# Moving the DRAM weight sums of a hybrid mLSTM / sparse-attention block from the projection strips into attention, in another order of steps

## The chip, the core and the metric

The kernel runs on one core of a Trainium2 chip. The metric is device time in microseconds of one execution; a measured kernel has several runs, and their median is compared. The engines are named as the profile names them: PE is the tensor engine (PEld its weight loads), DVE the vector engine, ACT the scalar engine, POOL the GpSimd engine. SP issues DMAs and computes nothing; POOL issues DMAs too, beside its own computing. Times in the stages are us from the start of the profiled span.

## The reference

One layer of a decoder block on x of 512 tokens by 1024 channels, all in fp32:

```python
hN = _rmsnorm(x, norm_g[l])
p = _split_in(hN @ w_in[l])          # one projection, cut into q, k, v, o, z, gates, ...
mh = _mlstm(silu(conv(p["m_q"])), silu(conv(p["m_k"])), p["m_v"], i_gate, f_gate)
ya = sigmoid(p["m_o"]) * _head_layernorm(mh) * silu(p["m_z"])
yb = _nsa(q, compressed, selected, window, gates) * silu(p["n_z"])
merged = sigmoid(p["g_a"]) * (ya @ w_branch_a) + sigmoid(p["g_b"]) * (yb @ w_branch_b)
x = x + merged @ w_out
return _rmsnorm(x, final_norm_g)
```

The mLSTM branch has 4 heads of 256; the attention branch has 8 query heads of 64 in 2 groups. What matters here is four products of a 512 x 1024 matrix with a 1024 x 1024 weight: the projections to v, o and z, and the last one with w_out.

## The kernel before, in words

Every fp32 operand of a product is split into a high and a low part, and a product is three matmuls (high x high, high x low, low x high). A weight goes by `weights()`: SP loads 512 KB of it into a raw tile `wr` of which there are three; ACT copies the high part into `wh` (also three), DVE subtracts and writes the low part `wl` (three). A raw buffer is loaded again when DVE is done with it, and a `wh` is written again when PE is done with it.

The four big products are made in a form of Strassen's: quarters of the weight are added and subtracted, so that seven products of quarters stand for eight. The sums of weight quarters are made by DMA in DRAM, with no engine computing. A sum has two steps, each of two DMAs of 512 KB: `begin_sum` (SP, line 929) copies a quarter of the weight into a DRAM tile, `wsumv1` to `wsumv4` for v, `wsumo1` to `wsumo4` for o, `wsumout1` to `wsumout4` for w_out. `add_to_sum` (POOL, line 935) then adds another quarter, or another sum, to it: sum 2 adds sum 1, and sum 4 adds sum 2. z's sums are made on DVE from tiles `E` and `F` instead.

The 24 steps are called chores and stand in one list, `chores`; the places in the program at which the next one is taken set where its DMAs stand in the queues of SP and POOL. A chore's DMAs are kept in program order among themselves and with other pinned instructions; instructions that are not pinned are put by the scheduler of the framework where it likes.

The stages, by the span of the profile:

- to about 93: norm, keys and values, first gates and convolutions; two chores are taken here.
- attention, about 93 to 272: 16 units (query pair, head, branch). A unit's scores are made on PE, exponentiated on ACT, scaled on POOL (tile `P`, five instructions a unit), transposed on PE and multiplied with the values. Between them PE is fed from a stream of projection jobs (queries, convolutions q and k, gates), each with one weight. One chore is taken at the start of each unit, in the units 0 to 13.
- the strips, about 272 to 398: the projections to v, o and z, in 21 products of quarters. PE is fed from weights alone here: 12 matmuls for a 512 KB weight. `Strip` names what is done after each product; a table `then` of o and z took four chores in all, after one product of o and three of z.
- the heads, about 398 to 520: four mLSTM heads, with branch products in the stream; one chore a head. POOL computes one small power `rlr` a head.
- the end, 520 to 600: merge, the product with w_out, norm and stores.

Of the kernel before, what the change touches and what calls it, by code (L numbers as in the profile page):

```python
# [89 lines left out]
def build(  # L90
# [3 lines left out]
    nc = tc.nc  # L94
# [717 lines left out]
    def query_heads(c):  # L812
        H, L, *turned = roped.pop(("q", c))
        q = rope_b(*turned)
        Th = []

        def part(hh):
            s = slice(hh * 64, hh * 64 + 64)
            o = slice((1 - hh) * 64, (1 - hh) * 64 + 64)
            t = rpp.tile([128, T], F32R, name="Th", tag=f"Th{hh}")  # L820
            A(t[s, :], q[s, :], AF.Copy)
            dve.tensor_tensor(t[o, :], q[s, :], f(t[s, :]), OP.subtract)
            Th.append(t)

        heads[c] = H, L, Th
        return part
# [91 lines left out]
    def quarters(w, c0):  # L918
        return [[w[:, 4 * i : 4 * i + 4, c0 + 512 * j : c0 + 512 * j + 512] for j in range(2)] for i in range(2)]

    wov = w_out[0].rearrange("(k p) c -> p k c", p=128)
    parts_of = {"v": quarters(wv, MV), "o": quarters(wv, MO), "z": quarters(wv, MZ), "out": quarters(wov, 0)}
# [15 lines left out]
    def chores_of(w):  # L938
        (b11, b12), (b21, b22) = parts_of[w]
        return [  # L940
            lambda: begin_sum(w, 1, b11),
            lambda: begin_sum(w, 3, b12),
            lambda: begin_sum(w, 2, b22),
            lambda: begin_sum(w, 4, b21),
        ], [
            lambda: add_to_sum(w, 1, b12),
            lambda: add_to_sum(w, 3, b22),
            lambda: add_to_sum(w, 2, wsum[w, 1]),
            lambda: add_to_sum(w, 4, wsum[w, 2]),
        ]  # L950

    begun, added = zip(*(chores_of(w) for w in ("v", "o", "out")))
    (c1, c3, c2, c4), (a1, a3, a2, a4) = begun[2], added[2]
    chores = deque(begun[0] + added[0] + begun[1] + added[1] + [c1, c2, a1, a2, c3, a3, c4, a4])

    def next_chore():
        chores.popleft()()
# [173 lines left out]
    def new_p():  # L1131
        return (
            at.tile([128, 1280], F32, name="P", tag="P", bufs=3),
            at.tile([128, 8, NT], F32, name="st", tag="st", bufs=4),
        )
# [22 lines left out]
    def turn(n, i, P, kbs):  # L1158
        c, hh, b = units[i]

        def job():
            for kb, tt in ptrans(P, kbs).items():
                applying.setdefault(n + AFTER[kb], []).append(lambda kb=kb, tt=tt: apply(c, hh, b, kb, tt))

        turning.setdefault(n, []).append(job)
# [12 lines left out]
    for i, (c, hh, b) in enumerate(units):  # L1178
        cur = pair[b]
        if b and i + 1 < 16:  # L1180
            pair = new_p(), new_p()
        if i % 4 == 2 and c < 3:
            while ("q", c + 1) not in roped:
                stream.step(1)
            now["rp"] = lambda c=c: now.__setitem__("th", query_heads(c + 1))
            now["c"] = lambda c=c: side.append(compressed(c + 1))
            at_place("u")
        if i == 0:
            side.append(mgate())
        if i < 14:  # L1190
            next_chore()
        for j, kbs in enumerate(((0,), (1,), (2, 3))):
            turn(n + LATER + j, i, cur[0], kbs)
        for g in range(NT):
            if i + 1 < 16:
                score(*units[i + 1], g, pair)
            for job in turning.pop(n, ()):
                job()
            for job in applying.pop(n, ()):
                job()  # L1200
            n += 1
            if g % 2 == 0:
                continue
            for w in PLACES[g]:
                at_place(w)
            for _ in range(4):
                tick(FILL)
# [22 lines left out]
    def vals(h):  # L1230
        return yah[:, h, : NT * 258].rearrange("p (b d) -> p b d", b=NT)
# [12 lines left out]
    gate = gtp.__enter__().tile([128, NT, D], F32, name="gate")  # L1244
# [15 lines left out]
    E = st.tile([128, 4, 512], F32, name="E")  # L1260

    def piece_of(src, q):
        return src[:, 2 * q : 2 * q + 2]
# [59 lines left out]
    F = {}  # L1323

    def z_first(q):
        nc.sync.dma_start(piece_of(E, q), piece_of(parts_of["z"][0][0], q))
        return halves_of(piece_of(E, q))

    def z_sum1(q):
# [155 lines left out]
    def fetch_decay(h):  # L1485
# [1 line left out]
        tc.keep_in_program_order(nc.sync.dma_start(decays["g", h], decayed[h].partition_broadcast(128)))  # L1487

    sv = Strip("v", put_values)
    so = Strip("o", put_o, lambda l: gate[:, l, 512:], {5: next_chore})  # L1490

    sz = Strip(
        "z", put_z, None,
        {
            1: next_chore,
            2: next_chore,
            5: lambda: fetch_qk(0, (0,)),
            6: lambda: [fetch_decay(h) for h in (0, 1)],
            3: next_chore,
            7: lambda: fetch_qk(0, (1,)),  # L1500
        },
    )
# [99 lines left out]
    for h in range(4):  # L1602
        (qh, ql), (kh, kl) = tiles_of[0, h], tiles_of[1, h]
        vh, vl = vals(h), vals_low(h)
        Dm = decays.pop(h)
        Sh = mp.tile([128, 1280], F32R, name="Sh", tag="Sh")
        Sl = mp.tile([128, 1280], F32R, name="Sl", tag="Sl")
        for sb in range(NT):
            o, n = KOFF[sb], 512 - sb * 128
            pss = PT() if sb < 2 else PS()  # L1610
            ss = slice(sb * 128, sb * 128 + 128)
            mm3(
                pss[:, :n], lambda k: kh[:, k, ss], lambda k: kl[:, k, ss],
                lambda k: qh[:, k, sb * 128 :], lambda k: ql[:, k, sb * 128 :], range(2),
            )
            dv = Dm[:, o : o + n]
            dve.scalar_tensor_tensor(dv, pss[:, :n], 0.015625, dv, OP.mult, OP.mult)
            split(dv, Sh[:, o : o + n], Sl[:, o : o + n])
        stream.step(24)
        if h < 3:  # L1620
            fetch_qk(h + 1)
            if h < 2:
                fetch_decay(h + 2)
        chores.popleft()()
        if h == 3:
            mqp.__exit__(None, None, None)
            fetch_first()
        num = mp.tile([128, NT, 258], F32, name="num", tag="num")
        bs = mp.tile([128, NT, 6], F32, name="bs", tag="bs")
        mv = mp.tile([128, NT, 2], F32, name="mv", tag="mv")  # L1630
        for tb in range(NT):
            po = PT() if tb < 2 else PS()
            for sb in range(tb + 1):
                a = KOFF[sb] + (tb - sb) * 128
                lh, ll = Sh[:, a : a + 128], Sl[:, a : a + 128]
                pe.matmul(po[:, :258], lh, vh[:, sb, :], start=sb == 0, stop=False)
                pe.matmul(po[:, :256], lh, vl[:, sb, :], start=False, stop=False)
                pe.matmul(po[:, :258], ll, vh[:, sb, :], start=False, stop=sb == tb)
            A(num[:, tb], po[:, :258], AF.Copy)
            dve.bn_stats(bs[:, tb], num[:, tb, 0:256])  # L1640
            dve.bn_aggr(mv[:, tb], bs[:, tb])
        stream.step(24)
        rho = mp.tile([128, NT], F32, name="rho", tag="rho")
        va = mp.tile([128, NT], F32, name="va", tag="va")
        A(rho, num[:, :, 256], AF.Abs)
        dve.tensor_tensor(rho, rho, em[:, :, h], OP.max)
        dve.reciprocal(rho, rho)
        dve.tensor_tensor(va, rho, rho, OP.mult)
        dve.tensor_tensor(va, va, mv[:, :, 1], OP.mult)
        dve.tensor_scalar(va, va, EPS, None, OP.add)  # L1650
        r = rsqrt(mp, va, NT, "rl")
        dve.tensor_tensor(rho, rho, r, OP.mult)
        nb = mp.tile([128, NT], F32, name="nb", tag="nb")
        dve.scalar_tensor_tensor(nb, mv[:, :, 0], -1.0, rho, OP.mult, OP.mult)
        for tb in range(NT):
            nt = num[:, tb, 0:256]
            A(nt, nt, AF.Identity, bias=nb[:, tb : tb + 1], scale=rho[:, tb : tb + 1])
            dve.tensor_tensor(nt, nt, gate[:, tb, h * 256 : h * 256 + 256], OP.mult)
        if h < 3:
            decay(h + 1)  # L1660
        stream.step(NORM_FILL)
        for e in range(2):
            pt = PT()
            for tb in range(NT):
                pe.transpose(
                    pt[:, tb * 128 : tb * 128 + 128], num[:, tb, e * 128 : e * 128 + 128], ident
                )
            ct = h * 2 + e
            gain = prm[:, ct, 10:11]
            A(ya(ct), pt, AF.Copy, scale=gain)  # L1670
            dve.scalar_tensor_tensor(yal[:, ct], pt, gain, f(ya(ct)), OP.mult, OP.subtract)
        stream.step(12)
# [321 lines left out]
```

## Time and profile before

| | us |
|---|---|
| median of 3 runs | 601.69 (600.55 to 602.02) |
| the profiled execution's own time | 602.6 |
| its span, first to last instruction | 600.5 |
| PE busy | 585.8 (98%) |
| DVE busy | 459.0 (76%) |
| ACT busy | 363.5 (61%) |
| POOL busy | 121.4 (20%) |
| mean granted clock | 0.995 |

A busy PE is not PE at its peak: matmuls overlap and their ends are modelled, so the start of one matmul to the start of the next tells more than its length. In a list of waits, "A <- B: 3.4, 1, 3.4" reads: A waited for B 3.4 us in total, once, 3.4 at the longest. In a row of the timeline stand start, length, engine, line, operation, what it writes and reads, how many instructions are merged in the row, and in brackets how long the engine idled before and what ended that. In a table of stretches, the DMA share is the mean busy share of the 16 DMA engines.

### The profile page before, as it was taken

Reading aid. Unit: us, or ns where it says so; the run is one execution under the profiler, and the core shown is the slowest. Engines: PE = TensorE matmul, PEld = TensorE weight load, DVE = VectorE, ACT = ScalarE, POOL = GpSimd, SP = SyncE. Lnnn points to the kernel's source line nnn. Section 1 sums busy time; section 2 is a strip of 40 time slices with the busy share of each in tenths; the row PEclk is TensorE's granted clock in tenths of the full one; section 3 lists DMA queues with packets and bytes.
Section 4 is the critical chain, followed back from the end, with each engine's and each line's share of the span. In section 5 each row is a group of like instructions: output and inputs, shape, how many; then the busy total and the mean of one; then the engine's idle time right before and its main releaser. Section 6 shows DMA issues by size and latency. Waiting matters only on the chain.

```text
span 600.5 us, 8563 instructions
## 1 busy us (share of the span) xinstructions
PE 585.8 (98%) x2896; PEld 491.5 (82%) x2896; DVE 459.0 (76%) x863; ACT 363.5 (61%) x662; POOL 121.4 (20%) x196
## 2 busy tenths in 40 slices
PE   8999999999999999999999799999999999999995
PEld 6898888888888888878888577888888888888884
DVE  4897669978869779887976376878767666679885
ACT  6848746676666667675765355576655542644544
POOL 5420601436323245440000110000200010001011
PEclk9999999999999999999999989999999999999999
DMA  8944995688993498874687886965996698767733
GB/s 319 330 115 134 279 245 146 194 197 197 229 260 111 134 225 180 202 170 130 220 278 231 227 204 188 300 178 164 335 271 224 207 276 265 246 205 260 239 103 141
DMA packets 102276, 128.47 MB, mean 214 GB/s; under 512 B 6228, under 2 KB 63188, under 8 KB 102232
## 3 DMA queue, kind: packets, MB, share of 16 engines
q1 hardware_dynamic: 96184, 112.78, 60.0%
q0 software_dynamic: 5760, 14.75, 14.5%
q8 instruction: 23, 0.38, 0.3%
q10 hardware_dynamic: 288, 0.39, 0.2%
q14 instruction: 21, 0.17, 0.1%
HBM read 109.61 MB, written 42.02 MB: 253 GB/s over the span
## 4 chain that ended last, share of the span: by engine, by line
PE 80%; DVE 9%; DMA 6%; ACT 4%; issue 2%; DVEq 0%; ACTq 0%
PE pp L234 11%; PE pp L232 11%; PE pp L230 11%; DMA wr<-w_in 4%; PE pp L1365 3%; PE pp L484 3%; PE pp L1367 3%; PE pp L1363 3%; PE pt L1097 2%; DVE wl L105 2%; PE pp L1720 2%; PE pp L1718 2%; PE pp L1722 2%; DMA wr<-wsumo 1%; DVE u L105 1%
## 5 line engine op out<-in xcount | busy, mean ns | idle before, releaser
L105 DVE TENSOR_TENSOR wl<-wr,wh 128x1024 fp32r<-128x1024 f32 (+3 forms) x103 | 122.3, 1190 | 58.5 <-ACT wh L105 57.3
L105 ACT ACTIVATE wh<-wr 128x1024 fp32r<-128x1024 f32 (+3 forms) x104 | 105.8, 1020 | 70.2 <-PE pp L232 18.0
L232 PE MATMUL pp<-hTl,wh 128*128 128x512 f32 x320 | 126.1, 394 | 0.0
L230 PE MATMUL pp<-hTh,wh 128*128 128x512 f32 x320 | 126.0, 394 | 0.0
L234 PE MATMUL pp<-hTh,wl 128*128 128x512 f32 x320 | 125.6, 393 | 0.0
L105 POOL TENSOR_SCALAR P<-P,st,gates 128x128 f32<-128x128 f32 (+2 forms) x80 | 53.5, 678 | 123.9 <-DVE st L105 117.3
L234 PEld LDWEIGHTS pp<-hTh,wl 128*128 128x128 f32 x320 | 60.1, 188 | 11.8 <-DVE wl L105 0.3
L230 PEld LDWEIGHTS pp<-hTh,wh 128*128 128x128 f32 x320 | 60.2, 188 | 11.3 <-ACT wh L105 0.2
L232 PEld LDWEIGHTS pp<-hTl,wh 128*128 128x128 f32 x320 | 60.2, 188 | 11.1
L105 ACT ACTIVATE P<-P,st 128x128 f32<-128x128 f32 (+3 forms) x64 | 35.6, 557 | 20.0 <-DVE st L105 19.7
L105 DVE SCALAR_TENSOR_TENSOR u<-pp,cst,u 128x511 f32<-128x511 f32 (+2 forms) x48 | 35.6, 741 | 1.5 <-ACT u L105 1.4
L105 ACT ACTIVATE pth<-pt 128x384 fp32r<-128x384 f32 (+1 forms) x48 | 24.9, 521 | 17.4 <-PE pt L1097 17.1
L105 DVE TENSOR_TENSOR ptl<-pt,pth 128x384 fp32r<-128x384 f32 (+1 forms) x48 | 28.4, 594 | 6.8 <-ACT pth L105 6.7
L105 DVE CUSTOM_DVE_ANT_0 P<-ps,cst 128x128 f32<-128x128 f32 (+3 forms) x64 | 30.2, 480 | 2.8 <-PE ps L1078 2.6
L105 POOL TENSOR_TENSOR rlr<-va,mhalf 128x4 f32<-128x4 f32 x4 | 4.1, 1032 | 137.7 <-DVE va L105 137.7
L1097 PE MATMUL pt<-cst,P 128*128 128x128 f32 x160 | 25.4, 273 | 0.0
L1097 PEld LDWEIGHTS pt<-cst,P 128*128 128x128 f32 x160 | 19.8, 140 | 4.4 <-DVE ptl L105 0.8
L1108 PE MATMUL po<-pth,vsw 128*128 128x512 f32 (+1 forms) x64 | 21.8, 350 | 0.8 <-ACT pth L105 0.6
L1363 PE MATMUL pp<-wh,S 128*128 128x512 f32 x48 | 19.5, 406 | 3.0 <-ACT wh L105 3.0
L1365 PE MATMUL pp<-wl,S 128*128 128x512 f32 x48 | 19.5, 406 | 1.7 <-DVE wl L105 1.7
L1367 PE MATMUL pp<-wh,S 128*128 128x512 f32 x48 | 19.4, 405 | 0.0
L1109 PE MATMUL po<-ptl,vsw 128*128 128x512 f32 (+1 forms) x64 | 19.3, 327 | 0.0
(429 smaller groups left out, 1408.0 us busy)
## 6 DMA issues: line engine op xcount, KB each, us to landing
wr<-w_in SPq DMA_DIRECT2D x60, 512.0 KB, 5.8
qk<-hl SPq DMA_DIRECT2D x16, 512.0 KB, 3.9
qk<-qk SPq DMA_DIRECT2D x16, 512.0 KB, 6.5
away<-s SPq DMA_DIRECT2D x16, 256.0 KB, 2.6
wsumv<-w_in SPq DMA_DIRECT2D x8, 512.0 KB, 7.0
wsumo<-w_in SPq DMA_DIRECT2D x8, 512.0 KB, 6.3
wr<-wsumv SPq DMA_DIRECT2D x8, 512.0 KB
wr<-wsumo SPq DMA_DIRECT2D x8, 512.0 KB, 6.5
```

Of the source, the lines that this page charges most:

```text
L105: ins = fn(*args, **kw)
L230: pe.matmul(ps, a, c, start=k == 0, stop=False)
L232: pe.matmul(ps, a, d, start=False, stop=False)
L234: pe.matmul(ps, b, c, start=False, stop=k == nk - 1)
L484: pe.matmul(keys_in[c], (b if p == 2 else a)[:, cs_], xl[k] if p == 1 else xh[k], start=k == 0 and p == 0, stop=k == ND - 1 and p == 2,)
L1097: pe.transpose(pt[:, n : n + 128], P[:, POFF[qb] + kb * 128 : POFF[qb] + kb * 128 + 128], ident)
L1108: pe.matmul(po[:, kb * 128 :], vl, th, start=b == 0 and kb == 0, stop=False)
L1109: pe.matmul(po[:, kb * 128 :], vl, tl, start=False, stop=False)
L1363: pe.matmul(ps, a, c, start=begin, stop=False, skip_group_check=not first)
L1365: pe.matmul(ps, a, d, start=False, stop=False, skip_group_check=not first)
L1367: pe.matmul(ps, b, c, start=False, stop=k == 3, skip_group_check=not first)
L1718: pe.matmul(ps, p, ya(k), start=k == 0, stop=False)
```

## The change

The list of chores is put in another order, and the places where a chore is taken change. In attention the units 1, 3, 5 and 7 take two, the others one, unit 15 none: 19 in place of 14. The strips take none. The heads take what is left, one each in the first three: the copy for w_out's sum 4, and the additions to its sums 2 and 4. In the list the additions for v, o and w_out stand mixed with the copies of the next weight. The two loads of `E` are pinned to program order.

```diff
     begun, added = zip(*(chores_of(w) for w in ("v", "o", "out")))
-    (c1, c3, c2, c4), (a1, a3, a2, a4) = begun[2], added[2]
-    chores = deque(begun[0] + added[0] + begun[1] + added[1] + [c1, c2, a1, a2, c3, a3, c4, a4])
+    (v1, v3, v2, v4), (o1, o3, o2, o4), (c1, c3, c2, c4) = begun
+    (va1, va3, va2, va4), (oa1, oa3, oa2, oa4), (a1, a3, a2, a4) = added
+    chores = deque(
+        [v1, v3, v2, v4, va1, va3, va2, o1, va4, o3, o2, o4, oa1, oa3, oa2, c1, oa4, c2, c3, a1, a3, c4, a2, a4]
+    )
...
-        if i < 14:
+        for _ in range(2 if i in (1, 3, 5, 7) else i < 15):
             next_chore()
...
     def z_first(q):
-        nc.sync.dma_start(piece_of(E, q), piece_of(parts_of["z"][0][0], q))
+        tc.keep_in_program_order(nc.sync.dma_start(piece_of(E, q), piece_of(parts_of["z"][0][0], q)))
...
-    so = Strip("o", put_o, lambda l: gate[:, l, 512:], {5: next_chore})
+    so = Strip("o", put_o, lambda l: gate[:, l, 512:])
...
-            1: next_chore,
-            2: next_chore,
             5: lambda: fetch_qk(0, (0,)),
             6: lambda: [fetch_decay(h) for h in (0, 1)],
-            3: next_chore,
             7: lambda: fetch_qk(0, (1,)),
...
-        chores.popleft()()
+        if chores:
+            next_chore()
```

On PE, DVE and ACT the instructions stand in the same order as before. On SP and POOL they don't; three places follow.

SP in the strips, from o's second product on (`wr` is a raw weight tile, `wsumo2` and its like the sums in DRAM, `E` z's first weights). Before:

```order
L170 DMA wr_3542<-wsumo2_2237 128x1024
L170 DMA wr_3562<-wsumo2_2237 128x1024
L929 DMA wsumout1_3583<-w_out 128x2x512 x2
L170 DMA wr_3586<-w_in 128x2x512
L170 DMA wr_3604<-w_in 128x2x512
L170 DMA wr_3625<-wsumo3_2120 128x1024
L170 DMA wr_3643<-wsumo3_2120 128x1024
L170 DMA wr_3665<-wsumo4_2365 128x1024
L170 DMA wr_3671<-wsumo4_2365 128x1024
L170 DMA wr_3741<-w_in 128x2x512
L170 DMA wr_3761<-w_in 128x2x512
L929 DMA wsumout2_3783<-w_out 128x2x512 x2
```

Now:

```order
L170 DMA wr_3555<-wsumo2_1860 128x1024
L170 DMA wr_3575<-wsumo2_1860 128x1024
L170 DMA wr_3596<-w_in 128x2x512
L170 DMA wr_3614<-w_in 128x2x512
L170 DMA wr_3635<-wsumo3_1857 128x1024
L170 DMA wr_3653<-wsumo3_1857 128x1024
L170 DMA wr_3675<-wsumo4_1983 128x1024
L170 DMA wr_3681<-wsumo4_1983 128x1024
L1329 DMA E_3154<-w_in 128x2x512 x2
L170 DMA wr_3751<-w_in 128x2x512
L170 DMA wr_3771<-w_in 128x2x512
```

Both copies for w_out are gone from here, and E's two loads, which stood among v's first loads, come behind o's last.

SP in attention, behind the turning of the third query pair (`rot1`; `away` and `qk` are stores of gates and of convolved q and k). Before:

```order
L320 DMA rot1_88<-rw_1772 8x512
L170 DMA wr_2101<-w_in 128x8x128
L929 DMA wsumo3_2120<-w_in 128x2x512 x2
L364 DMA away6944_0_1889<-s_1887 128x512
L929 DMA wsumo1_1974<-w_in 128x2x512 x2
L170 DMA wr_2205<-w_in 128x8x128
L170 DMA wr_2276<-w_in 128x8x128
L682 DMA qk01_1971<-hl_1968 256x1x512
```

Now:

```order
L320 DMA rot1_88<-rw_1777 8x512
L929 DMA wsumo3_1857<-w_in 128x2x512 x2
L929 DMA wsumo2_1860<-w_in 128x2x512 x2
L364 DMA away6944_0_1898<-s_1896 128x512
L929 DMA wsumo4_1983<-w_in 128x2x512 x2
L170 DMA wr_2110<-w_in 128x8x128
L170 DMA wr_2215<-w_in 128x8x128
L170 DMA wr_2285<-w_in 128x8x128
L682 DMA qk01_1980<-hl_1977 256x1x512
```

Three copies for o stand together, and the weight load that was ahead of them is behind them.

POOL from the last unit of attention into the heads (`P` the scaled scores, `yah` the values' ones, `rlr` a head's power). Before:

```order
L105 TENSOR_SCALAR P_2864<-P_2864,st_2865,gates_70 128x384
L105 TENSOR_SCALAR P_2866<-P_2866,st_2867,gates_70 128x128
L105 TENSOR_SCALAR P_2866<-P_2866,st_2867,gates_70 128x256
L105 TENSOR_SCALAR P_2866<-P_2866,st_2867,gates_70 128x384
L105 TENSOR_SCALAR P_2866<-P_2866,st_2867,gates_70 128x128
L105 TENSOR_SCALAR P_2866<-P_2866,st_2867,gates_70 128x384
L105 MEMSET yah_3113 128x4 x8
L935 DMA wsumout1_3583<-w_out 128x2x512 x2
L935 DMA wsumout2_3783<-wsumout1_3583 128x1024 x2
L105 TENSOR_TENSOR rlr_4347<-va_4340,mhalf_68 128x4
L935 DMA wsumout3_4252<-w_out 128x2x512 x2
L105 TENSOR_TENSOR rlr_4647<-va_4640,mhalf_68 128x4
```

Now:

```order
L105 TENSOR_SCALAR P_2875<-P_2875,st_2876,gates_70 128x384
L935 DMA wsumout3_2761<-w_out 128x2x512 x2
L105 TENSOR_SCALAR P_2877<-P_2877,st_2878,gates_70 128x128
L105 TENSOR_SCALAR P_2877<-P_2877,st_2878,gates_70 128x256
L105 TENSOR_SCALAR P_2877<-P_2877,st_2878,gates_70 128x384
L105 TENSOR_SCALAR P_2877<-P_2877,st_2878,gates_70 128x128
L105 TENSOR_SCALAR P_2877<-P_2877,st_2878,gates_70 128x384
L105 MEMSET yah_3126 128x4 x8
L105 TENSOR_TENSOR rlr_4350<-va_4343,mhalf_68 128x4
L935 DMA wsumout2_2635<-wsumout1_2374 128x1024 x2
L105 TENSOR_TENSOR rlr_4650<-va_4643,mhalf_68 128x4
L935 DMA wsumout4_4255<-wsumout2_2635 128x1024 x2
```

The additions for w_out's sums 1 and 3 are issued in attention (the one for sum 1 a unit earlier), the latter ahead of the last unit's scalings; the other two follow in the heads. Elsewhere in attention the additions for v and o stand earlier in POOL's queue than before, and o's first two, sums 1 and 3, stand next to each other behind unit 7's scalings, with the one for sum 2 behind unit 8's.

## The prediction

> **What bounds the kernel now.** I read the page's first part, then the busy times of each engine cut by stage (columns: stretch, length, busy us and instruction count of PE, PEld, DVE, ACT, POOL, then granted clock, DMA share, GB/s).
>
> ```profile
> PE 585.8 (98%) x2896; PEld 491.5 (82%) x2896; DVE 459.0 (76%) x863; ACT 363.5 (61%) x662; POOL 121.4 (20%) x196
> ...
> 95.00:275.00 180.00, 179.20 (x956) 151.14 (x955) 150.49 (x356) 119.86 (x267) 68.78 (x96) 1.00 0.74 181
> ...
> 340.00:350.00 10.00, 6.27 (x20) 4.48 (x19) 4.25 (x5) 4.01 (x6) 0.00 (x0) 0.83 0.62 191
> ...
> 372.00:376.00 4.00, 3.01 (x14) 2.15 (x13) 4.00 (x5) 2.66 (x4) 0.00 (x0) 1.00 0.38 86
> ...
> 400.00:520.00 120.00, 120.00 (x630) 103.09 (x628) 84.48 (x189) 64.22 (x126) 8.17 (x8) 1.00 0.84 255
> ```
>
> TensorE bounds nearly all of it. Attention (95 to 275) has 0.8 us of PE idle, the heads (400 to 520) none. The one hole is in the strips: 3.73 us at 340 to 350 with the clock at 0.83, and 0.99 us at 372 to 376. The order of instructions on PE, DVE and ACT is the same in both kernels; only SP and POOL issue in another order. So the change can give back what those holes cost and can take what it puts into attention, nothing else. What PE's weight loads waited for after 275, then PE's own rows around the holes, and the clock in the stretch behind the first:
>
> ```profile
> PEld pp L1363 <- ACT wh L105: 3.4, 1, 3.4
> PEld pp L1365 <- DVE wl L105: 2.5, 2, 1.4
> ```
> ```profile
> 335.62 0.39 PE L1363 MATMUL pt<-wh,S 128*128 128x512 f32 x1
> ...
> 340.86 0.39 PE L1367 MATMUL pp<-wh,S 128*128 128x512 f32 x1
> 344.23 0.50 PE L1363 MATMUL pp<-wh,S 128*128 128x512 f32 x1 [2.97 <-ACT wh L105]
> 345.49 0.55 PE L1365 MATMUL pp<-wl,S 128*128 128x512 f32 x1 [0.76 <-DVE wl L105]
> ...
> 349.24 0.40 PE L1365 MATMUL pp<-wl,S 128*128 128x512 f32 x1
> ...
> 373.03 0.39 PE L1363 MATMUL pp<-wh,S 128*128 128x512 f32 x1
> 374.41 0.50 PE L1365 MATMUL pp<-wl,S 128*128 128x512 f32 x1 [0.99 <-DVE wl L105]
> ```
> ```profile
> 345.81:349.22 3.41, 3.41 (x9) 2.67 (x8) 2.65 (x4) 1.86 (x3) 0.00 (x0) 0.50 0.71 167
> ```
>
> From 335.62 to 340.86 there are 23 steps, 5.24 / 23 = 0.228 us each: the undisturbed cadence of a 512-column matmul. At 340.86 it breaks, and once PE runs again, nine steps (345.49 to 349.24) go at half clock. What made the weights late is in the chain of waits (start, us, what):
>
> ```profile
> 324.31 7.60 DMA wr<-w_in
> 331.99 1.07 ACT wh L105
> 333.09 1.24 DVE wl L105
> 334.34 8.67 DMA wr<-wsumo
> ...
> 361.98 7.65 DMA wr<-w_in
> ```
>
> A weight buffer is loaded, split on ACT (1.07) and DVE (1.24), and there are three of them. Each holds 12 matmuls, 12 x 0.228 = 2.73 us of PE; three give 8.2 us a turn, so a load keeps up while it lands within 8.2 - 2.31 = 5.9 us. These landed in 7.6 to 8.7. How loads land without and with the weight sums (first row 285 to 321, second 321 to 345; the last figure is the median us to landing), and the sums' issues on SP and on POOL:
>
> ```profile
> wr<-wsumo SPq DMA_DIRECT2D x3, 512.0 KB, 4.4
> ...
> wr<-wsumo SPq DMA_DIRECT2D x5, 512.0 KB, 8.7
> ```
> ```profile
> 321.69 1.29 SPq L929 DMA_DIRECT2D wsumout<-w_out  x2
> 348.23 1.22 SPq L929 DMA_DIRECT2D wsumout<-w_out  x2
> ```
> ```profile
> 329.62 2.42 POOL L935 DMA_DIRECT2D wsumout<-w_out  x2 [51.34 <-DMA wsumout<-w_out]
> 355.03 0.83 POOL L935 DMA_DIRECT2D wsumout<-wsumout  x1 [22.99 <-DMA wsumout<-w_out]
> ```
>
> The load at 324.31 was issued 2.6 us behind the first copy, the loads at 334.34 and 361.98 4.7 and 7.0 us after POOL began a sum. That is the whole hole.
>
> **The change part by part.** *Strips.* Two copies and two sums leave 321 to 367. Freed of them, loads should land as at 285 to 321, in about 4.4, under 5.9. The cost that goes, term by term: 344.23 - 340.86 - 0.228 = 3.14; 345.49 - 344.23 - 0.228 = 1.03; nine steps at half clock, 3.75 - 9 x 0.228 = 1.70; 374.41 - 373.03 - 0.228 = 1.15. Sum **7.02 us**. Next to be late is nothing in the DMA: PE's own cadence. For the half clock, the Trainium skill ("TensorE: Matmul & The Clock Gate", Part 1) says that the array falls to half rate after an idle window of about 3.4 us and stays there for about one; the trace agrees (one stretch of 3.41 at 0.50). By that rule a hole that only shrinks below a window would lose no half clock, and the 1.70 would be kept even then.
>
> *E.* The 1 MB of z's first weights was fetched at 280 and is now issued behind the last load of o's sums, which stood at 337.58 of the old clock. Its row:
>
> ```profile
> E<-w_in SPq DMA_DIRECT2D x2, 512.0 KB, 4.7
> ```
>
> It lands near 343. PE, without the holes, wants it 43 matmuls after 340.86, at 350.7; less both splits (2.31), 348.4. Even at 8.7 it is in time. But it shares the engines with o's last loads, so I leave a residual of **0.3**. Its bounds are 0 and 4: the 55 us from 321 to 376 are 6.7 turns of 8.2, and each falls 0.6 short if loads land at the median that the page has for o's sums over the whole kernel, 6.5 rather than 5.9:
>
> ```profile
> wr<-wsumo SPq DMA_DIRECT2D x8, 512.0 KB, 6.5
> ```
>
> *Attention, DMA.* Three copies (3.15 MB) and two sums (2.1 MB) come in. The queues there and the weights:
>
> ```profile
> q1 hardware_dynamic: 24880, 24.03, 43.6%
> q0 software_dynamic: 3328, 8.39, 30.2%
> ...
> wr<-w_in SPq DMA_DIRECT2D x21, 512.0 KB, 4.8
> wsumo<-w_in POOLq DMA_DIRECT2D x4, 512.0 KB, 9.4
> ```
>
> 43.6% of 180 us for 24.03 MB is 3.27 us/MB, 30.2% for 8.39 MB is 6.48. So 3.15 x 3.27 + 2.1 x 6.48 = 23.9 us of 180: DMA share 0.74 to 0.87. The Trainium skill ("DMA: Bandwidth & Descriptors", Issuing engines are not separate DMA queues) speaks against the change: work issued from SP and from POOL ends on the same 16 engines, so moving it saves none. The trace agrees that both queues draw on one budget (43.6% and 30.2% make the 0.74).
>
> What decides is the room. In attention a weight is used every 180 / 21 = 8.6 us, so three buffers give 25.7 a turn where the strips give 8.2; 25.7 - 2.31 leaves 23 us for a landing, against 9.4 for a sum's own. Of the 30 waits listed for this stretch none has a DMA as releaser; ACT's weight splits wait for PE alone:
>
> ```profile
> ACT wh L105 <- PE pp L232: 7.7, 6, 1.8
> ```
>
> One load is moved directly: it stood ahead of o's copies and is now behind three of them and a store. The load, the store, and the split that I count as that load's own (loads and splits paired backward from the strips):
>
> ```profile
> 159.59 0.39 SPq L170 DMA_DIRECT2D wr<-w_in  x1
> ...
> 166.25 0.34 SPq L364 DMA_DIRECT2D away<-s  x1
> ...
> 183.04 1.05 ACT L105 ACTIVATE wh<-wr 128x1024 fp32r<-128x1024 f32 x1
> ```
>
> Issued near 168 and landing within 10 it is there at 178, 5 us early. Cost **0**; without that cover a late load costs its lateness.
>
> *Attention, POOL.* A pair of sum issues holds POOL 2.42 (row at 329.62). What queues behind it are P's scalings, for which PE's transposes wait.
>
> ```profile
> 184.01 1.09 POOL L105 TENSOR_SCALAR P<-P,st,gates 128x128 f32<-128x128 f32 x2 [0.83 <-DVE st L105]
> 193.16 2.69 POOL L105 TENSOR_SCALAR P<-P,st,gates 128x128 f32<-128x128 f32 x5 [8.06 <-DVE st L105]
> 205.43 2.15 POOL L105 TENSOR_SCALAR P<-P,st,gates 128x128 f32<-128x128 f32 x3 [9.58 <-DVE st L105]
> ...
> 265.80 3.49 POOL L105 TENSOR_SCALAR P<-P,st,gates 128x128 f32<-128x128 f32 x5 [1.56 <-DVE st L105]
> ```
>
> Four issues in a row now stand after 185.10: 4.84 into an idle 8.06, hidden with 3.2 over. Only the last sum, ahead of the last unit's scalings at 265.80, does not fit: POOL idles 1.56, the pair takes 2.42, so P is 0.86 late, and there PE has little else to fill with. The cost is between 0 (the first of the five took long anyway) and 0.9; I take **0.3**.
>
> *Heads.* Two copies and two sums become one copy and two sums. PE idles nowhere from 400 to 520 although two sums land there now: **0**, bounds 0 to 0.5.
>
> Sum: -7.02 + 0.3 + 0.3 = **-6.4**. Profiled: span 600.5, own time 602.6, so 594.1 and 596.2. The median of the runs is 601.69; on that, **595.3**.
>
> **Rivals.** *Half rescue.* The strips get lighter but loads still land near 6 to 7, since E moves in among o's last loads and z's fetches stay. For it: the 6.5 above. Against: 4.4 at 285 to 321, though F's 1 MB was fetched there. With 3 us of residual instead of 0.3 the sum is -7.02 + 3.0 + 0.3 = -3.7: **598**.
>
> *Attention takes it back.* The sums fill the DMA engines until weights come late. For it: the 0.74 that is there already. Against: 0.87 is still under 1, with 23 us of room for a landing. To come out as no change it must cost some 6 of the 7: 601.7 - 7.0 + 6.2 = **600.9**. The rule of the Trainium skill named above is the case for this one.
>
> *POOL blocks: slower.* The sum of o2 reads what the first of the four sums in a row wrote. In POOL's order it waits for that landing right after the scalings of 193.16 and holds back the next unit's. With a landing of 9.4 it waits not at all. The next unit's scalings start at 205.43; less 1.6 to issue the pair, a landing later than 203.8, which is 18.7 after 185.1, makes P late and PE with it. To end over 0.3% slower it must return 7.0 + 1.8 = 8.8 us: a landing 27.5 us after issue, three times the row. At 30 the price is 11.3, less 7.0: **606**.
>
> **How the numbers follow.** Forecast 79%, half rescue 11%, taken back 6%, slower 4%. 0.3% of 601.7 is 1.8 us, about what a measurement tells from no change: faster 0.90, same 0.06, slower 0.04. The gain's bounds: all 7.02 and a little of the run's spread gives 593.8; the high end reaches past the half rescue with its residual at the full 4, 599.
>
> **What would show it.** Right: PEld's waits after 275 lose the 3.4 and 2.5, no stretch at 0.50 behind them, o's loads land near 4.5, PE's share reaches 99%. Attention: no DMA among the releasers, POOL's idle at 193 shrinks to about 3, PE at 270 slips by under 1 us. Wrong: a hole with ACT wh <- DMA near E or z's weights (half rescue), PE idle between 185 and 275 with POOL P as releaser (the other two).

## The result, and the profile after

| | us |
|---|---|
| median of 14 runs | 596.11 (594.59 to 600.63) |
| the kernel before, beside it, median of 14 | 601.61 (600.11 to 602.38) |
| ratio | 0.9914, 95% interval 0.9895 to 0.9932 |
| the profiled execution's own time, its span | 594.59, 592.5 |

The kernel is faster by 5.5 us, by the interval 4.1 to 6.3. Predicted were 595.3, in 593.8 to 599.0. First the busy times of the profile after, and of its stretches those that were shown of before (columns as there: stretch, length, busy us and count of PE, PEld, DVE, ACT, POOL, granted clock with 1.00 for full speed, DMA share, GB/s).

```profile
PE 582.6 (98%) x2896; PEld 490.6 (83%) x2896; DVE 459.0 (77%) x863; ACT 363.3 (61%) x662; POOL 119.8 (20%) x196
```
```profile
95.00:275.00 180.00, 179.20 (x954) 151.19 (x954) 150.05 (x357) 119.93 (x266) 72.30 (x100) 1.00 0.86 210
...
340.00:350.00 10.00, 10.00 (x45) 8.06 (x44) 6.96 (x8) 6.28 (x9) 0.00 (x0) 1.00 0.71 247
372.00:376.00 4.00, 4.00 (x20) 3.30 (x19) 2.48 (x3) 2.61 (x3) 0.00 (x0) 1.00 1.03 288
400.00:520.00 120.00, 120.00 (x630) 103.06 (x629) 84.74 (x188) 64.58 (x122) 7.50 (x8) 1.00 0.78 235
```

Both holes are gone: 10.00 and 4.00 us busy where 6.27 and 3.01 were, at a clock of 1.00 where 0.83 stood. Attention is as full as before (179.20) though its DMA share went from 0.74 to 0.86, and the heads lost nothing. PE's share of the span, which was to reach 99%, stays at 98%. What PE's weight loads still wait for from 275 to the end, in full, and what ACT's weight splits wait for from 321 to 350, first before, then after:

```profile
PEld pp L1366 <- DVE part L105: 0.8, 3, 0.3
PEld pt L183 <- DVE yal L105: 0.3, 1, 0.3
```
```profile
ACT wh L105 <- DMA wr<-wsumo: 7.1, 2, 6.8
ACT wh L105 <- DMA wr<-w_in: 2.7, 2, 2.5
```
```profile
ACT wh L105 <- PE pp L1370: 3.7, 4, 1.2
ACT wh L105 <- PE pt L1370: 3.6, 3, 1.7
```

Before, the splits waited for loads; now they wait for PE to give a buffer back. A weight is ready before it is wanted, which is what "PE bounds the strips" looks like from the side of the loads.

Of the 8.0 us between the two spans (600.5 and 592.5), 7.2 lie between 340 and 380. This is the sum over PE's rows of the distance from start to start less the lower quartile of that distance for the same width: 7.5 before, 0.3 after. 0.5 more were lost ahead of 100 in before; the last section tells why that part differs from run to run, and why the medians are only 5.5 apart.

### The profile page after: what moved, and what is told of

Its sections match the earlier page's. It is cut to its first block, busy times and chain, and to the rows that moved or that the text cites. A ratio compares the mean times of both kernels' runs of the same rounds, so it can differ in the third digit from the quotient of the medians.

```text
span 592.5 us, 8564 instructions
## 1 busy us (share of the span) xinstructions
PE 582.6 (98%) x2896; PEld 490.6 (83%) x2896; DVE 459.0 (77%) x863; ACT 363.3 (61%) x662; POOL 119.8 (20%) x196
## 4 chain that ended last, share of the span: by engine, by line
PE 87%; DVE 6%; ACT 3%; DMA 2%; issue 1%; DVEq 0%; ACTq 0%
PE pp L234 12%; PE pp L230 12%; PE pp L232 12%; PE pp L1366 3%; PE pp L1368 3%; PE pp L1370 3%; PE pp L484 3%; PE pt L1100 2%; PE pt L1366 2%; PE pt L1368 2%; PE pt L1370 2%; PE pp L1719 2%; PE pp L1723 2%; PE pp L1721 2%; PE po L1111 1%; PE po L1112 1%
## 5 line engine op out<-in xcount | busy, mean ns | idle before, releaser
L1366 PE MATMUL pt<-wh,S 128*128 128x512 f32 x48 | 18.7, 389 | 0.0
L1368 PE MATMUL pt<-wl,S 128*128 128x512 f32 x48 | 18.7, 389 | 0.0
L1370 PE MATMUL pt<-wh,S 128*128 128x512 f32 x48 | 18.7, 389 | 0.0
```

The costliest lines, as they stand in the source:

```text
L1366: pe.matmul(ps, a, c, start=begin, stop=False, skip_group_check=not first)
L1368: pe.matmul(ps, a, d, start=False, stop=False, skip_group_check=not first)
L1370: pe.matmul(ps, b, c, start=False, stop=k == 3, skip_group_check=not first)
```

## Which part of the strips' work made the holes

The prediction called the two copies and the two sums together "the whole hole". Seven kernels take them apart. In each diff below, `nothing` is a chore that does nothing, put in the list for the one moved, so that the other chores keep their places (with the copies alone, the addition for sum 4 comes one head later).

**The first pair alone.**

```diff
-... oa3, oa2, c1, oa4, c2, c3, a1, a3, c4, a2, a4]
+... oa3, oa2, nothing, oa4, c2, c3, nothing, a3, c4, a2, a4]
-so = Strip("o", put_o, lambda l: gate[:, l, 512:])
+so = Strip("o", put_o, lambda l: gate[:, l, 512:], {5: c1})
 sz = Strip("z", ..., {
+    2: a1,
```

> The changed kernel with the first copy and the first sum of the output weights left in the strips where they stood (copy at o's fifth product, its sum as soon as the copy has landed); the second pair, the pinned E and the list stay as changed. My theory (each of the two holes is made by its own pair, and the half clock hangs on the first): the hole near 340 comes back whole, 3.14 + 1.03 + 1.70 = 5.9, the 1.15 at 373 does not: 596.1 + 5.9 = 602.0, as slow as before; with E now fetched in the same place up to 4 more. Rival, the pairs share the loss evenly: 596.1 + 3.5 = 599.6. Rival, it was E's place and not the sums that made the loads late: 596.1.

601.03 us, ratio to before 1.0007 (0.9979 to 1.0034): the whole gain is gone. PE's rows at the hole, and the loads in the chain of waits:

```profile
344.15 0.50 PE L1369 MATMUL pp<-wh,S 128*128 128x512 f32 x1 [2.35 <-ACT wh L105]
345.41 0.79 PE L1371 MATMUL pp<-wl,S 128*128 128x512 f32 x1 [0.76 <-DVE wl L105]
```
```profile
324.92 7.56 DMA wr<-w_in
...
334.91 8.02 DMA wr<-wsumo
```
```profile
340.00:350.00 10.00, 6.90 (x23) 5.07 (x23) 4.25 (x5) 4.19 (x6) 0.00 (x0) 0.83 0.91 318
```

It is the hole of before again, with the same two late loads (7.60 and 8.67 there) and the half clock, 3.11 us idle in place of 3.73. E, fetched beside them here, made it no worse.

**The second pair alone.**

```diff
-... oa3, oa2, c1, oa4, c2, c3, a1, a3, c4, a2, a4]
+... oa3, oa2, c1, oa4, nothing, c3, a1, a3, c4, nothing, a4]
 sz = Strip("z", ..., {
+    1: c2,
+    3: a2,
```

> The changed kernel with the second copy and the second sum left in the strips (copy at z's first product, sum when it has landed). My theory: only the hole at 373 comes back, 1.15, too short for half clock: 596.1 + 1.15 = 597.3. Rival, the pairs share the loss evenly: 599.6. Rival, E's place was the cause: 596.1.

595.02 us, 0.9913 (0.9881 to 0.9944): nothing came back, not even the 1.15. The strips from 350 to 380:

```profile
350.00:380.00 30.00, 30.00 (x134) 24.86 (x133) 23.49 (x23) 18.28 (x24) 1.38 (x2) 1.00 0.87 244
```

So the second hole was not the price of the second pair as such. Two loads stood beside the sum here too; they landed in 7.2 and 6.3 where before's took 8.4 and 7.65, soon enough for PE.

**The copies alone.** c1 and c2 stay at `{5: c1}` and `{1: c2}` in the strips, a1 and a2 go to the heads.

```diff
-... oa3, oa2, c1, oa4, c2, c3, a1, a3, c4, a2, a4]
+... oa3, oa2, nothing, oa4, nothing, c3, nothing, a3, c4, a1, a2, a4]
```

> Both copies stay in the strips, their two sums go to the heads (there one copy and three sums). In before, the load beside the first copy landed in 7.6 us and the next one of the same buffer, beside the sum, in 8.67: 16.3 where two turns at 5.9 allow 11.8, 4.5 too much for a hole of 3.1, so some 1.3 are cushion. My theory: with the copy alone it is 7.6 + 4.4 = 12.0, inside 11.8 + 1.3: no hole, 596.1 to 596.4. Rival, the copy is what matters: 602.

596.07 us, 0.9909 (0.9874 to 0.9943). ACT's splits did wait for loads, from 321 to 350, and PE did not notice:

```profile
ACT wh L105 <- DMA wr<-wsumo: 2.9, 2, 1.7
...
ACT wh L105 <- DMA wr<-w_in: 2.3, 2, 2.0
```
```profile
340.00:350.00 10.00, 10.00 (x45) 8.07 (x44) 7.87 (x9) 6.01 (x8) 0.00 (x0) 1.00 0.98 345
```

A DMA share of 0.98 over ten microseconds did no harm. With both sums in the heads, the copies did not have to leave the strips.

**The sums alone, in four runs.** POOL has nothing else to do in the strips, so a sum runs as soon as its copy has landed, wherever it stands in the program. To hold it back, POOL first reads something that the strip has just written (`mark` is a scratch tile for that):

```diff
-... oa3, oa2, c1, oa4, c2, c3, a1, a3, c4, a2, a4]
+... oa3, oa2, c1, oa4, c2, c3, nothing, a3, c4, nothing, a4]
+def after_write(src, chore):
+    def run():
+        mark = yap.tile([128, 1], F32, name="mark", tag="mark")
+        tc.keep_in_program_order(pool.tensor_scalar(mark, src(), 0.0, None, OP.mult))
+        chore()
+    return run
 so = Strip("o", ..., {6: after_write(lambda: so.part(1)[:, 0, 0:1], a1)})
 sz = Strip("z", ..., {2: after_write(lambda: gate[:, 1, 0:1], a2), ...
```

> Both sums stay in the strips at about their old times (each behind a small POOL operation that reads what the strip has just written), their copies are done in attention as in the changed kernel. My theory, same arithmetic: 4.4 + 8.67 = 13.1 against 11.8 + 1.3 = 13.1, so a hole of 0 to 0.5 and no half clock: 596.1 to 596.6. Rival, the sums alone are the cause and the copies cost nothing: the holes come back whole, 596.1 + 7.0 = 603.

606.21 us, 1.0076 (1.0045 to 1.0106), slower than before and than either expectation, and two holes:

```profile
348.08 0.51 PE L1369 MATMUL pp<-wh,hTh 128*128 128x512 f32 x1 [0.39 <-ACT wh L105]
...
386.27 0.49 PE L1371 MATMUL pp<-wl,S 128*128 128x512 f32 x1 [2.89 <-DVE wl L105]
```

These sums came 5 and 15 us later than those of before (334.93 and 369.69), beside E and beside the heads' first fetches, so two more runs put them back to their old places, one with E at 280 as before, one with E pinned:

```diff
-{6: after_write(lambda: so.part(1)[:, 0, 0:1], a1)}
+{5: after_write(lambda: so.part(2)[:, 1, 0:1], a1), 4: after_write(lambda: gate[:, 3, 0:1], a2)}
 # in z's table:
-    2: after_write(lambda: gate[:, 1, 0:1], a2),
 # and, in the first of the two:
-tc.keep_in_program_order(nc.sync.dma_start(piece_of(E, q), ...))
+nc.sync.dma_start(piece_of(E, q), ...)
```

> The changed kernel with both sums in the strips, at the places they had before (behind small POOL operations: the first when o's fifth product is stored, near 329, the second when o's last is, near 351), the copies in attention, and E not pinned, so that it is fetched at 280 as before. Against before only the copies are gone from the strips. Turn arithmetic of the earlier expectations: 4.4 + 8.67 = 13.1 against 13.1, a hole of 0 to 0.5: 596.1 to 596.6. Rival, the sum alone makes the hole (two sums with E beside them cost 10 where they stood 5 and 15 us later): 596.1 + 5.9 = 602 or more.

> The same with E pinned behind o's last load, as in the changed kernel. If E beside a sum is what made the loads of the later sums land in 9 to 11 us, this one shows a hole near 345 of 1 to 3 and the run with E at 280 none: 597 to 599 against 596. If the sum alone does it, both are equal, near 602. If only the later time did it, both are near 596.

603.17 us, 1.0030 (0.9998 to 1.0061), and 602.36 us, 1.0010 (0.9980 to 1.0040): equal, and as slow as before. It is not E and not the later time. But all three runs had something else too: PE stepped more slowly through most of the strips from 297 on, 0.233 us from one 512-column matmul to the next and not 0.227. The tile `mark` had moved all that is allocated behind it by 32 bytes, so one more run, with E at 280, made it 64 bytes wide.

```diff
-mark = yap.tile([128, 1], F32, ...)
+mark = yap.tile([128, 16], F32, ...)     # POOL writes mark[:, 0:1]
```

> The run with both sums at their old places in the strips and E at 280, once more, with one size changed: the scratch tile that POOL's small operations write is 64 bytes wide and not 4. The 4-byte tile moved every tile behind it in SBUF by 32 bytes; in both runs with it PE's 512-column steps took 0.233 us from 300 to 400 and not 0.227, 2.1 + 1.3 + 0.4 less what the changed kernel shows there, 0.1 + 1.0 + 0.0, so 2.7 in all. If the address is the cause, the cadence is 0.227 again and the time 603.2 - 2.7 = 600.5, with the holes of some 4.5 us still there: then the sums alone make the holes. Rival, the waiting POOL operation slows PE: cadence 0.233, 603. Rival, the shifted addresses also made the loads late: no holes, 596.

602.61 us, 1.0005 (0.9980 to 1.0030). PE's rows over 32 steps in this run, then its holes and the load that came last at the first:

```profile
303.32 0.39 PE L1371 MATMUL pp<-wl,S 128*128 128x512 f32 x1
...
310.79 0.39 PE L1369 MATMUL pt<-wh,S 128*128 128x512 f32 x1
...
343.95 0.50 PE L1369 MATMUL pp<-wh,S 128*128 128x512 f32 x1 [1.60 <-ACT wh L105]
345.21 0.50 PE L1371 MATMUL pp<-wl,S 128*128 128x512 f32 x1 [0.76 <-DVE wl L105]
...
373.32 0.50 PE L1371 MATMUL pp<-wl,S 128*128 128x512 f32 x1 [0.64 <-DVE wl L105]
```
```profile
334.93 10.57 DMA wr<-wsumo
```

7.47 / 32 = 0.233: the cadence is still slow, so it does not hang on the 32 bytes as such. The last section tells which matmuls are slow in these four kernels; it costs them some 2.7 us, an estimate, and must be taken off before they are compared: 602.6 - 2.7 = 599.9, still 3.8 above the changed kernel. That is about what the trace shows as holes. Five distances between PE's starts there (1.99, 1.26, 0.79, 0.60 and 1.03, less 0.23 each) make 4.5 us; in before the same reckoning gives 5.3, and 1.7 of half clock.

So **the sums make holes without the copies, and the copies make none without the sums**. A load beside a sum alone lands in 10.6 here, one beside the first copy in 7.6 (rows of before and of the first pair). The expectation that both were needed, each half of what one raw buffer can bear, fell. Whether a copy lengthens a hole that a sum makes stays open: the first wait is 2.97 in before and 1.60 here.

## What the other places cost

**Attention, by leaving the work out.** From the kernel before, the strips' four chores are dropped; nothing is moved.

```diff
-chores = deque(begun[0] + added[0] + begun[1] + added[1] + [c1, c2, a1, a2, c3, a3, c4, a4])
+chores = deque(begun[0] + added[0] + begun[1] + added[1] + [c3, a3, c4, a4])
+wsum["out", 1], wsum["out", 2] = parts_of["out"][0][0], parts_of["out"][1][1]
```

> The kernel before with the strips' two copies and two sums left out (the sums of the output weights are then only the raw weights, and the output is not the reference's); attention, its list and E at 280 as before. It is the strips' gain without a price in attention. My theory: 601.6 - 7.0 = 594.6 at best, and attention's price in the changed kernel is what the changed kernel is above this run: 0.3 + 0.3 predicted, so 595.5 with the run's spread. Rival, attention costs 2 to 3 of the 7 that the strips gave back (the medians differ by 5.5 only): 593 to 594.

596.26 us, 0.9916 (0.9879 to 0.9954); the changed kernel has 596.11. With the work gone altogether the time is that of the kernel in which it was moved: attention takes it for nothing, within the 2 us that these intervals leave. PE is busy throughout from 340 to 350 here too, at a DMA share of 0.61.

**E's place.** The changed kernel without the pin on E's two loads, which then stand at 280 again.

```diff
-tc.keep_in_program_order(nc.sync.dma_start(piece_of(E, q), ...))
+nc.sync.dma_start(piece_of(E, q), ...)
```

> The changed kernel with E not pinned: it is fetched at 280 again. My theory: E's place is worth 0.3 at most in either direction: 595.8 to 596.4. Rival, beside o's last loads E takes 0.5 to 1.5: 594.6 to 595.6. Rival, at 280 it delays v's loads: 597 or more.

596.00 us, 0.9911 (0.9879 to 0.9942): the pin is worth nothing that these runs can tell, in either direction.

**The mixed order.** The changed kernel with the list as it was, one weight after the other.

```diff
-[v1, v3, v2, v4, va1, va3, va2, o1, va4, o3, o2, o4, oa1, oa3, oa2, c1, oa4, c2, c3, a1, a3, c4, a2, a4]
+[*begun[0], *added[0], *begun[1], *added[1], c1, c2, c3, a1, a3, c4, a2, a4]
```

> The changed kernel with the list in the old order (each sum directly followed by the one that reads it), everything else as changed; v's second and fourth sum now fall into one step of attention. In the changed kernel the second sum is issued at 140.43 and lands at 154.24; here the fourth would stand right behind it on POOL, wait until then and hold back the scalings of 146.53 by 8 to 9. My theory: PE has little to fill that with, +4 to +9: 600 to 605. Rival, the stall is hidden as other waits on POOL are: 596.1.

595.60 us, 0.9887 (0.9858 to 0.9916): no slower. POOL did stand still as expected:

```profile
140.40 1.71 POOL L935 DMA_DIRECT2D wsumv<-wsumv  x2
149.74 0.81 POOL L935 DMA_DIRECT2D wsumv<-wsumv  x1 [7.63 <-DMA wsumv<-wsumv]
152.16 0.82 POOL L935 DMA_DIRECT2D wsumv<-wsumv  x1 [1.61 <-DMA wsumv<-wsumv]
152.73 3.34 POOL L105 TENSOR_SCALAR P<-P,st,gates 128x128 f32<-128x128 f32 x5
```

The five scalings start 6.2 later than in the changed kernel (146.53), and PE loses some 0.8 us by it: no matmul starts from 160.51 to 161.41. In the middle of attention P has slack of 5 us and more; there the order of the sums decided nothing.

**All in attention.** The last three chores are taken there as well; the heads get none.

```diff
-... c1, oa4, c2, c3, a1, a3, c4, a2, a4]
+... c1, oa4, c2, c3, a1, c4, a3, a2, a4]
-for _ in range(2 if i in (1, 3, 5, 7) else i < 15):
+for _ in range(2 if i in (1, 3, 5, 7, 9, 11, 13) else i < 15):
```

> All chores of the output weights in attention, none in the heads (22 of 24 in attention, two in every second step). It adds one copy (1.05 MB x 3.27) and two sums (2.1 MB x 6.48), 17.0 us of DMA time, to 180: share 0.86 to 0.95. My theory: landings stay far under the 23 us of room and no sum stands directly behind the one it reads: 595.8 to 597. Rival, near a full share the weights come late: 598 to 602, with weight splits that wait for a DMA.

604.50 us, 1.0051 (1.0025 to 1.0076): 8.4 above the changed kernel, and not for the reason that either theory gave. No weight split waits for a DMA in a way that reaches PE. It is POOL, in front of the last unit:

```profile
258.83 2.60 POOL L935 DMA_DIRECT2D wsumout<-wsumout  x2
265.69 3.13 POOL L105 TENSOR_SCALAR P<-P,st,gates 128x128 f32<-128x128 f32 x5 [4.25 <-DVE st L105]
274.64 0.82 POOL L935 DMA_DIRECT2D wsumout<-wsumout  x1 [5.82 <-DMA wsumout<-wsumout]
277.58 0.81 POOL L935 DMA_DIRECT2D wsumout<-wsumout  x1 [2.11 <-DMA wsumout<-wsumout]
278.14 2.90 POOL L105 TENSOR_SCALAR P<-P,st,gates 128x128 f32<-128x128 f32 x5
```
```profile
278.93 2.02 PE L1100 MATMUL pt<-cst,P 128*128 128x128 f32 x4 [5.78 <-POOL P L105]
```
```profile
279.00:282.50 3.50, 3.30 (x12) 2.49 (x13) 0.69 (x1) 0.70 (x2) 2.04 (x4) 0.50 1.04 184
```

Sum 4 reads sum 2, which was issued at 258.83 as the last of four in a row and was not all in DRAM until 277. POOL waits 7.9 for it, the last unit's scalings wait behind POOL, and PE waits 5.8 for those and then runs at half clock. Nothing is left in attention to fill with.

**All in the heads.** All eight chores of w_out two by two in the heads, 14 chores in attention.

```diff
-... oa2, c1, oa4, c2, c3, a1, a3, c4, a2, a4]
+... oa2, oa4, c1, c2, a1, c3, a2, c4, a3, a4]
-for _ in range(2 if i in (1, 3, 5, 7) else i < 15):
+for _ in range(i < 14):
-if chores:
-    next_chore()
+for _ in range(2):
+    next_chore()
```

> All eight chores of the output weights in the heads, two in each of the four steps; attention has 14 as before, the strips none. Against the changed kernel three copies and two sums (10.3 + 13.6 = 23.9 us of DMA time) come to the 120 us of the heads: share 0.78 to 0.98. My theory: there is no room left there, weights come late: 597 to 602. Rival, the heads take it as attention did: 596.

610.32 us, 1.0128 (1.0094 to 1.0162), worse than the worst expected. PE's two largest waits from 400 on, a load in the chain that led to the first, the split that waited for it, and the stretch around it:

```profile
PEld pt L183 <- DVE yal L105: 6.9, 1, 6.9
PEld pt L1640 <- issue: 3.8, 1, 3.8
```
```profile
444.79 16.73 DMA wr<-w_branch_b
```
```profile
462.68 1.23 DVE L105 TENSOR_TENSOR wl<-wr,wh 128x1024 fp32r<-128x1024 f32 x1 [5.83 <-ACT wh L105]
```
```profile
440.00:470.00 30.00, 23.54 (x115) 19.94 (x114) 17.63 (x40) 14.05 (x28) 2.75 (x3) 0.89 0.89 273
```

A weight that lands 16.7 us after its issue stops PE here, at a DMA share of 0.89, and it does so by way of DVE: DVE waits for the split of that weight, and the `yal` that PE needs stands behind it in DVE's order. In attention a share of 0.86, with loads that land in 16 and 17 beside four sums, stopped nothing. So the share alone does not tell. That a weight lasts less long in the heads fits (17 loads in their 120 us, 21 in attention's 180), but no run varies that by itself: the load was also issued later than in the changed kernel (438.30), behind two copies.

None of the twelve is faster than the changed kernel by more than the intervals; the lowest are 595.02 with the second pair left in the strips and 595.60 with the list in the old order. So, as far as moving one thing at a time tells, the change's whole worth lies in one step of it, the first sum that left the strips.

## Why the prediction was right, and where it was not

- **What bounds the kernel, and the 7.02.** Right: the profiled holes went as summed, with PE's own cadence behind them. One term in it was not what it was said to be. The 1.15 at 373 was put down to the second pair, but that pair put back alone costs nothing (595.02). The first pair brings back 4.9 (601.03; 5.6 by the two ratios to before, 1.0007 and 0.9914) where its terms make 5.9. The second hole hung on how sum and loads happened to meet.
- **"A load keeps up while it lands within 5.9".** Loads that land within it keep PE waiting nowhere here, but a few beyond it are cushioned: 7.2 and 6.3 beside the second sum cost PE nothing. The step that failed is the one that put the first copy, by the load at 324.31, beside the sums as a cause of the hole: with copies alone ACT waits for such a load about as long as before (2.3 and 2.7), and PE does not wait.
- **The half clock.** Its 1.70 went with the hole. That the trace agrees with a wholly idle window was misread: the 3.41 is the length of the slow stretch, and in the 3.41 us ahead of it (342.40 to 345.81) PE was busy for 0.83. The length of the hole does not say whether half clock comes: see the last section.
- **E, residual 0.3.** Nothing was found: no weight load waits for a DMA, and with E at 280 the time is the same (596.00).
- **Attention's DMA, cost 0.** Right. A share of 0.87 was worked out and 0.86 measured; left out altogether, the work saves nothing (596.26). The Trainium skill ("DMA: Bandwidth & Descriptors", Issuing engines are not separate DMA queues) has the traffic end on the same engines from wherever it is issued. The share agrees, and it cost nothing while there was room. One sign came out otherwise: two DMAs are among the releasers in attention now, where none was expected (POOL waits 4.5 us for v's sum 2, DVE 3.1 for a turned query). Neither reached PE.
- **Attention's POOL, 0.3.** Too high: no cost is seen. The four issues in a row and what follows them, and the pair ahead of the last unit's scalings:

```profile
184.45 4.64 POOL L935 DMA_DIRECT2D wsumo<-w_in  x4
192.57 2.69 POOL L105 TENSOR_SCALAR P<-P,st,gates 128x128 f32<-128x128 f32 x5 [3.48 <-DVE st L105]
...
263.60 2.25 POOL L935 DMA_DIRECT2D wsumout<-w_out  x2
265.24 3.47 POOL L105 TENSOR_SCALAR P<-P,st,gates 128x128 f32<-128x128 f32 x5
```

  The idle 8.06 shrank to 3.48, where 3.2 was worked out. The last scalings started at 265.24 and not later than before (265.80).
- **Heads, 0.** Right, with little to spare: three copies and two sums more, and they cost 14 us.
- **The rivals.** Half rescue and the share of the DMA engines did not come. What spoke for half rescue was a median of 6.5 over the eight loads of o's sums, but the profile gives a landing for two of them only, 4.4 ahead of the sums and 8.7 beside one; no load is known to have landed at 6.5. The one given 4%, POOL blocked behind a landing, is real: all chores in attention is just that, one unit from the end. Its price was set for the middle of attention, where P's slack of 5 us hides most of it (the list in the old order), and not for the end, where nothing does. In the changed kernel too POOL waits for v's sum 2, 2.44 and 2.02 us ahead of issues at 151.68 and 154.52, and PE does not notice.
- **The sum.** -6.4 predicted, -5.5 between the medians (-4.1 to -6.3), -8.0 between the two profiled executions. Neither residual was found. Without them the sum is -7.02 and misses the medians by 1.5, so a part of how near it came is luck. The half clock may be too large a term for a median: of 74 runs of the kernel before beside the experiments, 37 at a mean clock of 0.993 to 0.996 have a median of 601.0, and 15 at 0.998 or more 600.2, so it may not come in every execution. These runs have no profile that could show it.

## What to carry to other kernels

When loads come late, ask which transfer beside them lets them land late before moving all of them: here the accumulating DMAs made holes alone, and the plain copies of the same weights were harmless where they stood. Do not go by the DMA share alone: look at how long a load takes to land and at what stands behind the split that waits for it. Loads that landed after 16 us did nothing in attention, and one stopped PE in the heads. A transfer that waits for another one belongs neither in front of the last work of its queue nor one unit before a stage ends; in the middle the same wait was all but free.

## What the runs showed of the hardware

**Half clock goes by how busy PE was in a window of a fixed grid, not by the length of a hole.** Two runs that differ only in E's place had nearly the same hole: 1.53 and 0.77 us idle with E pinned, 1.76 and 0.76 with E at 280. The first of these waits, with E pinned, and two stretches of 3.41 us, up to the half clock and in it:

```profile
343.63 0.49 PE L1369 MATMUL pp<-wh,S 128*128 128x512 f32 x1 [1.53 <-ACT wh L105]
```
```profile
341.72:345.13 3.41, 1.11 (x4) 0.42 (x3) 1.51 (x2) 1.06 (x1) 0.00 (x0) 1.00 1.04 366
345.13:348.54 3.41, 3.41 (x9) 2.63 (x9) 2.74 (x4) 2.54 (x4) 0.00 (x0) 0.50 0.91 319
```

The same with E at 280:

```profile
343.59 0.50 PE L1369 MATMUL pp<-wh,S 128*128 128x512 f32 x1 [1.76 <-ACT wh L105]
```
```profile
340.12:343.54 3.42, 1.71 (x8) 1.04 (x6) 0.00 (x0) 1.06 (x1) 0.00 (x0) 1.00 1.02 313
343.54:346.95 3.41, 2.60 (x10) 1.93 (x11) 3.03 (x4) 1.70 (x3) 0.00 (x0) 1.00 0.42 97
```

The shorter hole got the half clock. Where the windows stand can be read from the traces. With E pinned, half clock sets in at 345.13 and again at 597.72, behind PE's last work: 252.59 us, which is 74 times 3.413. In before it is the same 74 (345.81 and 598.40), and in all six profiles that have more than one such start the distances are whole multiples of 3.413. With E at 280 the only start is at 596.12, and 74 such steps back is 343.54. So an edge of the grid cut this hole in two, and neither window was empty enough. Over the 14 profiles, half clock stood behind every window of the grid in which PE was busy for up to 0.42 of the time, behind 2 of the 14 windows with 0.47 to 0.65, and behind none with more.

The Trainium skill ("TensorE: Matmul & The Clock Gate", Part 1, What's actually happening) says that the gate looks at a window of about 3.4 us that runs free of the program. The traces agree, by the 3.413. That a whole window must be idle does not fit: with E pinned the window had 1.11 us of work in it.

**A part of why runs of one kernel differ by 2 us.** Near 78.7 a weight is loaded whose landing differs from run to run, 5.3 us after issue in the changed kernel's profile and 7.3 in the run with the copies. It shows in ACT's wait for it and in PE's at 93, here in the run with the copies; the changed kernel has neither:

```profile
85.97 1.06 ACT L105 ACTIVATE wh<-wr 128x1024 fp32r<-128x1024 f32 x1 [1.24 <-DMA wr<-w_in]
...
93.35 0.30 PE L791 MATMUL ps<-w2t,u 128*64 128x64 f32 x2 [1.24 <-ACT rw L105]
```

The changed kernel's profiled execution is its fastest, 594.59, and has no such wait; ten of the other thirteen profiles have one, of 0.2 to 1.7. In the profile with all chores in attention the wait is 1.73, and half clock follows it (0.50 from 96 to 100); with all in the heads it is 1.70, and none follows. Two of the changed kernel's 14 runs took 599.54 and 600.63 at a mean clock of 0.991, where the others have 0.997 to 0.999. That this is the same hole with half clock behind it is likely but not shown, since those runs have no profile.

**An accumulating DMA lands later as more stand in a row**: the four issued from 184.45 on landed 7.0, 10.1, 13.0 and 15.4 us after their issue, and loads beside them in 16.0 and 17.4.

**A slower step for tiles that were moved.** In the four kernels with `mark` not all 512-column matmuls step at 0.233; only some tiles do. In the run with the 64-byte tile, rows some 200 us behind POOL's last operation on `mark` (356.77), at a granted clock of 1.00:

```profile
554.84 0.40 PE L1857 MATMUL ps<-wh,m 128*128 128x512 f32 x1
...
560.21 0.39 PE L1859 MATMUL ps<-wh,m 128*128 128x512 f32 x1
...
562.51 0.39 PE L1857 MATMUL pt<-wh,hTh 128*128 128x512 f32 x1
...
568.40 0.39 PE L1859 MATMUL pp<-wh,hTl 128*128 128x512 f32 x1
```

The first two are 23 steps apart, 5.37 / 23 = 0.233, the last two 26 steps, 5.89 / 26 = 0.227. Those that read `S`, `m` or `mx` are slow, which are allocated behind `mark` and were moved by it; those that read `hTh`, `hTl`, `yah` or `yal`, allocated ahead of it, keep 0.227 in the same run. So it goes with the place of the tile that is read and not with POOL, which has long been done. Moves of 32 and of 64 bytes do the same; what it is about the place that matters is open.
